# Attention row minima of the scores, held as minus SCALE times themselves, as the bias of the exponential

## The chip, the core and the metric

The kernel runs on one core of one Trainium2 chip. The metric is the device time of one execution, in microseconds (us). A core has engines that run side by side and wait for each other by semaphores: TensorE (PE, with its weight loads as PEld), VectorE (DVE), ScalarE (ACT), GpSimd (POOL) and the queue SP that issues DMAs.

## The reference, cut to what matters

A decoder trunk of two layers, 512 positions, width 1024. Each layer has three parallel mixers (an SSD scan, an S5 scan, and multi-head latent attention). The change touches the attention alone, in which each of 16 heads computes:

```python
sc = (einsum('bqhd,bkhd->bhqk', qn, k_nope) + einsum('bqhr,bkr->bhqk', qr, k_r)) * scale   # scale = 96 ** -0.5
sc = where(kpos[None, :] <= qpos[:, None], sc, NEG_INF)
pr = softmax(sc, axis=-1)
o  = einsum('bhqk,bkhd->bqhd', pr, v)
```

## The kernel before, in words

`mla` works through 16 heads in order. For a head, `attend_qk` makes the scores in four query blocks of 128 rows; by causality block qb has (qb + 1) x 128 keys. Each block is three matmuls into a PSUM bank (`mm3`, lines 61 to 63, tile `aux`), then one reduction on VectorE (line 612) that adds the mask `cmask`, writes the scores to the SBUF tile `sc`, and accumulates the row maximum into one column of `mx`. In the trace the reduction is a custom operation followed by a short read of its accumulator. After four blocks, one VectorE operation (line 617, through the helper at line 73) makes `nm` = -SCALE x `mx`, and four exponentials on ScalarE (line 619, helper at line 66) turn `sc` into exp(SCALE x sc + nm), with the row sums into `rs`.

`attend_v` follows for the same head: ten transposes on TensorE (line 634), evictions that split each result into a high part on ScalarE (`ph`) and a low part on VectorE (`pl`, helper line 78), and the matmuls with the values (lines 644 to 647). `values` then halves and adds (tile `tmp`) and, for each second head, multiplies with the gate (`keep` from `tmp` and `keep`, line 78).

Between the heads the loop also issues the next pair's query and key projections (weights are split into `wh` on ScalarE and `wl` on VectorE or GpSimd; `qh`, `ql`, `kh`, `kl` are splits of results) and steps of `s5_prep` through `fill`. The latter keep GpSimd in runs of products (`pw`, `pv`, helper line 81) and TensorE in small matmuls (`pm`, `pM`, `pk`).

Tiles in PSUM are few: `aux` has three banks for scores, transposes and values together. The order on each engine isn't the order of the text: a planner (`schedule_with_timeline_sim=True` at the end of the file) places each instruction by priority in the order of the text and by its own simulated times, and the engines then run these lists in order. `align` reserves pad columns, so that tiles behind it start at chosen places; tiles are padded to 32 bytes a partition.

Of the kernel before, what the change touches and what calls it, by code (L numbers as in the profile page):

```python
# [9 lines left out]
F32 = mybir.dt.float32  # L10
F32R = mybir.dt.float32r
I32 = mybir.dt.int32
AF = mybir.ActivationFunctionType
ALU = mybir.AluOpType
# [6 lines left out]
P = 128  # L21
# [4 lines left out]
SCALE = 96.0 ** -0.5  # L26
# [8 lines left out]
class Trunk:  # L35
# [563 lines left out]
    def attend_qk(self, mp, q, k, h):  # L599

        nc = self.nc
        mx, nm = (mp.tile([P, 4], F32, name=x, tag=x, bufs=2) for x in ("mx", "nm"))
        if h == 0:
            self.align(mp, 32)
        scs = []
        for qb in range(4):
            n = (qb + 1) * P
            qs = slice(qb * P, qb * P + P)
            ps = self.bank()
            self.mm3(ps[:, :n], q[0][0:96, qs], q[1][0:96, qs], k[0][0:96, :n], k[1][0:96, :n], True, True)  # L610
            sc = mp.tile([P, n], F32, name=f"sc{qb}", tag=f"sc{qb}", bufs=2)
            nc.vector.tensor_tensor_reduce(  # L612
                out=sc, in0=ps[:, :n], in1=self.cmask[:, 512 - n:512], op0=ALU.add, op1=ALU.max,
                scale=1.0, scalar=-3.0e38, accum_out=mx[:, qb:qb + 1],
            )
            scs.append(sc)
        self.ts(nm, mx, -SCALE, None, ALU.mult)
        for qb, sc in enumerate(scs):
            self.act_(sc, sc, AF.Exp, scale=SCALE, bias=nm[:, qb:qb + 1], accum_out=self.rs[:, qb, h:h + 1])
        return scs  # L620

    def attend_v(self, mp, scs, v):
# [604 lines left out]
```

## Time and profile before

| what | before |
| --- | --- |
| median of 3 runs | 2001.6 us (2001.11, 2001.6, 2006.5) |
| the profiled execution, its own time | 1999.34 us |
| its span, first to last instruction | 1997.5 us |
| TensorE busy | 1883.4 us, 94% |
| VectorE busy | 1448.1 us, 72% |
| ScalarE busy | 941.1 us, 47% |
| GpSimd busy | 645.6 us, 32% |
| mean granted TensorE clock | 0.965 of full |

The profile is of one execution. Busy time is the time in which an engine ran an instruction; the granted clock is the share of TensorE's full clock (2.4 GHz) that the chip allowed, and its other level is 0.5 (1.2 GHz). In the timeline a bracket behind an instruction gives the time for which its engine had been idle, and what ended that.

### The profile page before, as it was taken

The page shows a single profiled execution, that of the slowest core. Times are in us where ns is not written, and L with a number is a line of the kernel's source. Part 1 is how long each engine was busy: PE and PEld are TensorE (multiplying, and loading weights), DVE is VectorE, ACT ScalarE, POOL GpSimd, SP SyncE. Part 2 cuts the span into 40 slices and gives each one's busy share as a digit, 9 for nine tenths or more (in the row PEclk, how much of TensorE's full clock was granted, in tenths as well). Part 3 has the DMA queues.
Part 4 walks back from the last instruction along what each step waited for, and adds up shares of the span by engine and source line. Part 5 has one row for each costly group of instructions (what it writes and reads, how often), then busy time and mean ns, then how long its engine had stood idle before and what let it go on. Part 6 is the DMA issues. An engine that isn't in the chain of part 4 may idle for free.

```text
span 1997.5 us, 27806 instructions
## 1 busy us (share of the span) xinstructions
PE 1883.4 (94%) x9688; PEld 1530.5 (77%) x9688; DVE 1448.1 (72%) x2845; ACT 941.1 (47%) x1743; POOL 645.6 (32%) x743
## 2 busy tenths in 40 slices
PE   7897999899999989999998999998999999999998
PEld 5685777687887778888876777776878887788887
DVE  6866667699999857744579666677999996666443
ACT  4364556522555545543333655564235563555431
POOL 1855467301233201201118556672013331012010
PEclk9898999899999999999998999998999999899999
DMA  5333244232312266345223333342232224662541
GB/s 159 94 115 86 88 116 121 74 120 81 131 64 73 70 172 182 106 132 177 96 84 88 112 104 111 91 140 83 96 122 78 75 74 111 182 173 85 166 130 42
DMA packets 132605, 219.96 MB, mean 110 GB/s; under 512 B 36208, under 2 KB 75760, under 8 KB 131952
## 3 DMA queue, kind: packets, MB, share of 16 engines
q1 hardware_dynamic: 132464, 218.19, 36.0%
q8 instruction: 76, 1.25, 0.2%
q14 instruction: 65, 0.53, 0.1%
HBM read 182.08 MB, written 31.33 MB: 107 GB/s over the span
## 4 chain that ended last, share of the span: by engine, by line
PE 59%; DVE 24%; DMA 8%; POOL 3%; ACT 3%; issue 2%; SPq 1%; DVEq 0%; POOLq 0%; ACTq 0%
PE mm L116 13%; PE mm L117 13%; PE mm L119 12%; DVE wl L78 4%; DMA wf<-in_w_in 3%; DVE keep L69 3%; PE mm L61 2%; PE mm L62 2%; PE mm L63 2%; DVE ms L894 2%; DVE sc_t L891 2%; PE pk L385 2%; DVE ms L893 1%; PE aux L61 1%; PE aux L62 1%
## 5 line engine op out<-in xcount | busy, mean ns | idle before, releaser
L116 PE MATMUL mm<-hh,wh 128*128 128x512 f32 (+1 forms) x1232 | 500.9, 407 | 16.0 <-DVE ql L78 8.8
L117 PE MATMUL mm<-hl,wh 128*128 128x512 f32 (+1 forms) x1232 | 493.5, 401 | 0.0
L66 ACT ACTIVATE wh<-wf 128x1024 fp32r<-128x1024 f32 (+1 forms) x294 | 291.4, 994 | 422.9 <-PE mm L117 232.7
L78 DVE TENSOR_TENSOR wl<-wf,wh 128x1024 fp32r<-128x1024 f32 (+1 forms) x243 | 297.0, 1227 | 180.6 <-ACT wh L66 151.9
L119 PE MATMUL mm<-hh,wl 128*128 128x512 f32 (+1 forms) x1232 | 315.4, 393 | 3.8 <-DVE wl L78 3.8
L116 PEld LDWEIGHTS mm<-hh,wh 128*128 128x128 f32 (+1 forms) x1232 | 237.3, 193 | 77.9 <-DVE ql L78 9.9
L117 PEld LDWEIGHTS mm<-hl,wh 128*128 128x128 f32 (+1 forms) x1232 | 236.7, 192 | 50.0 <-issue 1.9
L119 PEld LDWEIGHTS mm<-hh,wl 128*128 128x128 f32 (+1 forms) x1232 | 227.7, 187 | 53.3 <-DVE wl L78 4.6
L81 POOL TENSOR_TENSOR mg<-mg,tmp 128x512 f32<-128x512 f32 x32 | 77.4, 2420 | 461.4 <-DVE tmp L78 244.0
L81 POOL TENSOR_TENSOR wl<-wf,wh 128x1024 fp32r<-128x1024 f32 (+1 forms) x51 | 109.0, 2138 | 291.2 <-PE mm L119 185.9
L116 PE MATMUL mm<-ah,wh 128*128 128x512 f32 x512 | 200.6, 394 | 0.0
L117 PE MATMUL mm<-al,wh 128*128 128x512 f32 x512 | 199.8, 391 | 0.0
L119 PE MATMUL mm<-ah,wl 128*128 128x512 f32 x512 | 127.6, 390 | 0.0
L116 PEld LDWEIGHTS mm<-ah,wh 128*128 128x128 f32 x512 | 96.5, 189 | 21.6 <-issue 1.8
L117 PEld LDWEIGHTS mm<-al,wh 128*128 128x128 f32 x512 | 96.3, 188 | 20.6 <-DVE keep L78 0.5
L119 PEld LDWEIGHTS mm<-ah,wl 128*128 128x128 f32 x512 | 95.7, 188 | 19.5
L612 DVE CUSTOM_DVE_ANT_0 sc<-aux,cmask 128x128 f32<-128x128 f32 (+3 forms) x128 | 60.3, 485 | 50.2 <-PE aux L63 48.4
L81 POOL TENSOR_TENSOR pv<-pq,ar 128x288 f32<-128x288 f32 x64 | 56.7, 906 | 86.3 <-PE pk L385 69.8
L66 ACT ACTIVATE sc<-sc,nm 128x128 f32<-128x128 f32 (+3 forms) x128 | 70.3, 553 | 28.7 <-DVE nm L73 28.7
L78 DVE TENSOR_TENSOR pl<-aux,ph 128x512 fp32r<-128x512 f32 (+1 forms) x96 | 54.7, 593 | 25.6 <-ACT ph L66 25.2
L69 DVE SCALAR_TENSOR_TENSOR keep<-mm,cw,keep 128x511 f32<-128x511 f32 (+2 forms) x96 | 71.0, 740 | 2.1 <-ACT keep L66 1.5
L66 ACT ACTIVATE tmp<-mm 128x512 f32<-128x512 f32 x76 | 44.8, 593 | 58.5 <-PE mm L63 32.3
(344 smaller groups left out, 4083.4 us busy)
## 6 DMA issues: line engine op xcount, KB each, us to landing
wf<-in_w_in SPq DMA_DIRECT2D x156, 512.0 KB
odr<-pv SPq DMA_DIRECT2D x64, 128.0 KB
wf<-in_w_c SPq DMA_DIRECT2D x16, 512.0 KB
wf<-in_w_a SPq DMA_DIRECT2D x16, 512.0 KB
wf<-kpad SPq DMA_DIRECT2D x128, 64.0 KB
wf<-odr SPq DMA_DIRECT2D x16, 512.0 KB
wf<-in_w_glu SPq DMA_DIRECT2D x16, 512.0 KB
wf<-in_w_b SPq DMA_DIRECT2D x16, 512.0 KB
```

Of the source, the lines that this page charges most:

```text
L61: mm(out, ah, bh, start=start, stop=False)
L62: mm(out, ah, bl, start=False, stop=False)
L63: mm(out, al, bh, start=False, stop=stop)
L66: self.nc.scalar.activation(out, in_, func, **kw)
L69: self.nc.vector.scalar_tensor_tensor(out, in0, s, in1, op0, op1)
L78: self.nc.vector.tensor_tensor(out, a, b, op)
L81: self.nc.gpsimd.tensor_tensor(out, a, b, op)
L116: mm(ps[:m], wh[:, o(i)], bh, start=i == 0, stop=False)
L117: mm(ps[:m], wh[:, o(i)], bl, start=False, stop=False)
L119: mm(ps[:m], wl[:, o(i)], bh, start=False, stop=i == k - 1)
L385: nc.tensor.matmul(pk.rearrange("p g k -> p (g k)"), bbp[b % 2][:, q:q + 4].rearrange("p g h -> p (g h)"), v1[:, :, 0:8].rearrange("p g k ...
L612: nc.vector.tensor_tensor_reduce(out=sc, in0=ps[:, :n], in1=self.cmask[:, 512 - n:512], op0=ALU.add, op1=ALU.max, scale=1.0, scalar=-3.0e3 ...
```

## The change

The reduction at line 612 now takes the minimum of -SCALE x (score + mask) and writes the scores scaled in that way. The row minima (`mn`) are the bias that the exponential needs, so the operation that made `nm` is gone, and the exponential's scale is -1. `mn` has eight columns, of which four are used; the pad behind it grows from 32 to 48 columns.

```diff
     def attend_qk(self, mp, q, k, h):
 
         nc = self.nc
-        mx, nm = (mp.tile([P, 4], F32, name=x, tag=x, bufs=2) for x in ("mx", "nm"))
+
+        mn = mp.tile([P, 8], F32, name="mn", tag="mn", bufs=2)
         if h == 0:
-            self.align(mp, 32)
+            self.align(mp, 48)
         scs = []
         for qb in range(4):
             n = (qb + 1) * P
@@ -610,13 +611,12 @@
             self.mm3(ps[:, :n], q[0][0:96, qs], q[1][0:96, qs], k[0][0:96, :n], k[1][0:96, :n], True, True)
             sc = mp.tile([P, n], F32, name=f"sc{qb}", tag=f"sc{qb}", bufs=2)
             nc.vector.tensor_tensor_reduce(
-                out=sc, in0=ps[:, :n], in1=self.cmask[:, 512 - n:512], op0=ALU.add, op1=ALU.max,
-                scale=1.0, scalar=-3.0e38, accum_out=mx[:, qb:qb + 1],
+                out=sc, in0=ps[:, :n], in1=self.cmask[:, 512 - n:512], op0=ALU.add, op1=ALU.min,
+                scale=-SCALE, scalar=3.0e38, accum_out=mn[:, qb:qb + 1],
             )
             scs.append(sc)
-        self.ts(nm, mx, -SCALE, None, ALU.mult)
         for qb, sc in enumerate(scs):
-            self.act_(sc, sc, AF.Exp, scale=SCALE, bias=nm[:, qb:qb + 1], accum_out=self.rs[:, qb, h:h + 1])
+            self.act_(sc, sc, AF.Exp, scale=-1.0, bias=mn[:, qb:qb + 1], accum_out=self.rs[:, qb, h:h + 1])
         return scs
```

## Rows read from the trace of the kernel before

**Rows 1.** The page, part 1: busy us of each engine, share, instructions.

```profile
PE 1883.4 (94%) x9688; PEld 1530.5 (77%) x9688; DVE 1448.1 (72%) x2845; ACT 941.1 (47%) x1743; POOL 645.6 (32%) x743
```

**Rows 2.** Windows: stretch, length, busy us (instructions) of each engine, clock, DMA.

```profile
250.00:390.00 140.00, 129.02 (x662) 103.16 (x661) 96.15 (x200) 84.08 (x209) 86.04 (x130) 0.91 0.37 106
390.00:1000.00 610.00, 595.48 (x3111) 484.45 (x3111) 458.54 (x834) 271.83 (x404) 111.84 (x67) 0.99 0.37 116
```

**Rows 3.** Tile nm: ns shortest/median/longest; idle us, times; line: busy us, mean ns.

```profile
L73 DVE TENSOR_SCALAR nm<-mx x32: 150/171/4473, 117.9 to 1357.1; 128x4 f32<-128x4 f32 x32
...
  DVE nm L73: 28.7, 15
...
L73 DVE TENSOR_SCALAR nm<-mx 128x4 f32<-128x4 f32 x32 | 23.2, 724 | 0.2
```

**Rows 4.** Timeline, head 15 of layer 0: start us, us, engine, operation, [idle before].

```profile
371.98 3.19 DVE L73 TENSOR_SCALAR nm<-mx 128x4 f32<-128x4 f32 x1
...
374.51 0.63 POOL L81 TENSOR_TENSOR pw<-pbb,ar 128x256 f32<-128x256 f32 x1
...
375.82 0.58 PE L645 MATMUL aux<-pl,v 128*64 128x384 f32 x1 [2.32 <-DVE pl L78]
```

**Rows 5.** Timeline, head 15 of layer 1.

```profile
1357.07 3.20 DVE L73 TENSOR_SCALAR nm<-mx 128x4 f32<-128x4 f32 x1
...
1360.92 0.39 PE L645 MATMUL aux<-pl,v 128*64 128x384 f32 x1 [2.79 <-DVE pl L78]
```

**Rows 6.** Timeline, head 12 of layer 0; the last row is layer 1.

```profile
324.72 1.02 DVE L73 TENSOR_SCALAR nm<-mx 128x4 f32<-128x4 f32 x1
...
325.77 0.40 ACT L66 ACTIVATE sc<-sc,nm 128x128 f32<-128x128 f32 x1 [1.24 <-DVE nm L73]
...
327.97 0.84 ACT L66 ACTIVATE ph<-aux 128x512 fp32r<-128x512 f32 x2
...
329.33 0.39 PE L645 MATMUL aux<-pl,v 128*64 128x384 f32 x1 [1.00 <-DVE pl L78]
...
1315.29 0.39 PE L645 MATMUL aux<-pl,v 128*64 128x384 f32 x1 [1.01 <-DVE pl L78]
```

**Rows 7.** Windows at half clock behind the TensorE gaps of rows 4 to 6.

```profile
331.40:338.20 6.80, 6.62 (x20) 5.19 (x21) 6.57 (x19) 4.42 (x13) 3.50 (x6) 0.50 0.34 95
...
375.80:379.20 3.40, 3.38 (x16) 3.28 (x16) 2.86 (x7) 3.21 (x10) 0.15 (x1) 0.50 0.09 31
1317.80:1321.20 3.40, 3.40 (x10) 2.27 (x10) 3.34 (x8) 2.09 (x8) 1.13 (x2) 0.51 0.43 159
1362.20:1369.00 6.80, 6.71 (x23) 4.37 (x22) 4.17 (x9) 5.05 (x14) 0.59 (x2) 0.50 0.04 9
```

**Rows 8.** Lines by shape; tile sc (ns shortest/median/longest); TensorE's waits (us, times, longest).

```profile
L66 ACT ACTIVATE sc<-sc,nm 128x512 f32<-128x512 f32 x32 | 22.7, 710 | 0.0
...
L612 DVE CUSTOM_DVE_ANT_0 sc<-aux,cmask x128: 273/484/692, 112.9 to 1355.5; 128x128 f32<-128x128 f32 x32, 128x256 f32<-128x256 f32 x32, 128x384 f32<-128x384 f32 x32, 128x512 f32<-128x512 f32 x32
...
L69 DVE SCALAR_TENSOR_TENSOR keep<-mm,cw,keep 128x511 f32<-128x511 f32 x32 | 23.7, 740 | 1.5 <-ACT keep L66 1.5
...
PE aux L634 <- DVE mx L612: 6.9, 6, 2.5
```

**Rows 9.** Gate products on VectorE: tile keep; TensorE's timeline behind two held ones.

```profile
L78 DVE TENSOR_TENSOR keep<-tmp,keep x16: 682/1056/4871, 150.7 to 1372.0; 128x512 f32<-128x512 f32 x16
...
156.39 0.80 PE L116 MATMUL mm<-hh,wh 128*128 128x512 f32 x1 [4.25 <-DVE ql L78]
...
1253.96 0.69 PE L634 MATMUL aux<-ident,sc 128*128 128x128 f32 x2 [2.52 <-DVE mx L612]
```

**Rows 10.** Timeline, the longest nm (head 5 of layer 1), GpSimd and VectorE.

```profile
1183.18 4.47 DVE L73 TENSOR_SCALAR nm<-mx 128x4 f32<-128x4 f32 x1
...
1186.93 0.69 POOL L81 TENSOR_TENSOR pv<-bc,ai 128x288 f32<-128x288 f32 x1
...
1187.90 1.21 DVE L78 TENSOR_TENSOR wl<-wf,wh 128x1024 fp32r<-128x1024 f32 x1
```

## The prediction

> **What bounds the kernel now.** I read the engine totals first [rows 1]: TensorE is busy 94% of the span, VectorE 72%, ScalarE 47%. A shorter VectorE or ScalarE list is therefore worth something only where TensorE stands still. Next the stretches by stage [rows 2]: outside attention TensorE is busy 595.48 of 610.00 us, but in the second half of layer 0's attention it is idle for 140.00 - 129.02 = 11.0 us, and its mean granted clock is 0.91 of full. The whole change lies in attention, so the question is which of those idle microseconds belong to the step that goes.
>
> That step is `nm`, the 128x4 scaling of the row maxima, 32 times (16 heads, two layers). The answer for that tile [rows 3] is the main reading: the median is 171 ns, the shortest 150 ns, the longest 4473 ns; ScalarE stood idle for 28.7 us until one of them ended. A 128x4 operation has no reason of its own to take 4 us. The timeline around the longest ones tells why [rows 4, 10]: `nm` reads and writes SBUF, GpSimd was in an unbroken run of `pw` and `pv` products, and `nm` ended as one of the last of them ended (375.14 against 375.17; 1187.62 against 1187.65). The score reduction, which has one input in PSUM, shows no such stretching: the longest of its 128 takes 692 ns, for the largest shape [rows 8]. Of the 23.2 us that `nm` takes in all [rows 3], 32 x 0.171 = 5.5 are medians; the other 17.7 are waits, at 14 of the 32 places.
>
> One rule can be weighed against this. The Trainium skill, "SBUF — State Buffer", section "SBUF: two separate sides", says that VectorE and GpSimd take a shared port pair by an exclusive lock for a whole instruction, and that an operation with two SBUF inputs contends as well. The kind of wait agrees with the trace, its length less so: the 3.19 us of [rows 4] outlast several GpSimd instructions of 0.6 to 0.8 us, where the page's rule would give one. By one GpSimd instruction for each of 14 holds the whole effect would be at most 14 x 0.7 = 9.8 us of VectorE time, an estimate; the rows give 17.7.
>
> **The change part by part.**
>
> *`nm` goes.* Where does TensorE wait for it? Following each hold to the next idle entry of TensorE I find four places.
> - Head 15, layer 0 [rows 4]: `nm` sits ahead of `pl` on VectorE, and TensorE's values matmul waits 2.32 us for `pl`. Without `nm`, `pl` can start when its hi part is written, and the wait closes.
> - Head 15, layer 1 [rows 5]: the same order, 2.79 us.
> - Head 12, layers 0 and 1 [rows 6]: ScalarE's first exponential waits 1.24 us for `nm`; behind the four exponentials stands the `ph` eviction (327.97), and TensorE waits 1.00 and 1.01 us for what follows. The 1.24 us cover the 1.00.
> Sum: 2.32 + 2.79 + 1.00 + 1.01 = 7.1 us. The other ten holds have no TensorE gap of their own: the largest, 4.47 us [rows 10], ran beside matmuls that had their operands, so I count it at nothing. What covers it are projections; with those gone it would cost up to 4.47.
>
> What is late next? At head 15 the transposes need the exponentials, which now start behind `nm`; free of it they start when ScalarE has done its evictions, some 3 us sooner, and take at most 4 x 0.71 = 2.8 us [rows 8]. I allow 1 us of the 7.1 to come back there, as the lower end (6.1).
>
> *The clock.* Each of these gaps lies in or just ahead of a stretch at granted clock 0.50, that is 1.2 instead of 2.4 GHz [rows 7]. TensorE did 6.62 + 3.38 + 3.40 + 6.71 = 20.1 us of work in the four; at full clock that is half, so up to 10.1 us hang on the gaps. Other idle entries stand close by (the `pM` and `pml` waits of head 12 and 15), so some of these stretches can stay. Ends: 0 and 10.1. I take the middle, 5.0, since nothing in the trace says which of two neighbouring gaps lowered the clock.
>
> *The reduction with min and a scale of -SCALE.* The trace has no such reduction. It has the same custom operation with max and a scale of 1, up to 692 ns; the nearest two-step operation with a PSUM input and a per-partition factor takes 740 for 128x511 [rows 8]. So 0 to +50 ns each, 128 instructions, at most 6.4 us of VectorE time. TensorE waited six times, 6.9 us, for these reductions at line 634 [rows 8]: 6 x 0.05 = 0.3 us. A gain has no ground, as the operation count stays. I take 0: the multiply already stands in the old instruction, by 1.0.
>
> *The exponentials* keep form, count and an immediate scale: 0, plus or minus nothing that a row would show. They depend on one reduction now where `nm` made each wait for all four. This can move three of four ahead of the last reduction, off the block on ScalarE that delayed `ph` in [rows 6]. In heads 1 to 14 it is hidden by the projection and `s5_prep` matmuls that lie between a head's exponentials and its transposes; I count nothing beyond the 1.00 above. A new wait takes the place of the old: the exponential on its own reduction. Behind it on ScalarE stand the same `ph` and `wh` evictions as behind `nm`, and the reduction ends before `nm` did, so the wait is no longer than now.
>
> *The pad* (48 for 32 columns) only restores the place of the tiles behind it: two tags of two buffers become one, and it moves no work. I cost it at 0.
>
> *Order.* The planner places instructions from its own simulated times, so a dropped step and earlier exponentials can reorder the four engines through attention. I take 0 for it, and its ends, 13.6 us less and 20 us more, come from rivals D and C below.
>
> Sum against the profiled execution: 1999.3 - 7.1 - 5.0 = 1987.2. That execution was 2.3 us under the median of 2001.6, so the same gain from the median gives 1989.5. With the ends: 1995.5 (6.1 and no clock) to 1984.4 (7.1 and 10.1).
>
> **The rivals.**
>
> *B, the wait passes on.* VectorE's next instructions with two SBUF inputs meet the same GpSimd runs. For: the `wl` split follows soon behind the 4.47 us hold [rows 10], and the products of attention output and gate (`keep` from `tmp` and `keep`) are held as long as 4.87 us [rows 9]. Against: at head 15 the next on VectorE are two `pl`, which read PSUM. If only head 12 gains, with its clock half used, it is 2.0 + 2.5 less than now, about 1997; if nothing, 2001.6. By the Trainium skill's section above, with its lock on operations with two SBUF inputs, this would be the outcome.
>
> *C, slower: a new order lays the gate products into GpSimd's runs.* Place: the 16 products of [rows 9] that close a pair of heads. Five of 16 are now held for over 3 us, three in layer 0 and two in layer 1, though both layers run the same code; so the draw does move with order. Price: the first and the last of the five TensorE waits behind them are 4.25 and 2.52 us [rows 9], in the middle 3.4, and a half-clock stretch of 6.8 us [rows 7] costs 3.4 more: 6.8 each. Two more held ones eat the 12.1 us; three more give 1989.5 + 20.4 = 2010. It decides from three on.
>
> *D, the same draw the other way.* Two of the five go free: 1989.5 - 13.6 = 1976.
>
> That the change doesn't do what it says (exponentials still placed behind the fourth reduction) costs nothing here: all 7.1 us come from `nm` itself, and this falls within the first case.
>
> **How the numbers follow.** A change of 0.3%, 6.0 us, is about what a measurement of this kernel can tell from none; faster is under 1995.6, slower over 2007.6. Chances: A, the forecast, 0.43, at 1989.5 (own range 1984 to 1995.5, all faster); B 0.27, at 1997 to 2002, within 0.3%; C 0.20, at 2010, slower; D 0.10, faster. So faster 0.53, same 0.27, slower 0.20. The range runs from 1977, which leaves out half of D, to 2010, which leaves out half of C: 0.15 left out. Cases of both signs hold chance, so the own range of A stands beside it.
>
> **What would show it.** Right: no `nm`; VectorE busy about 23 us less; the 2.3 and 2.8 us entries of TensorE at head 15 and the 1.0 us ones at head 12 gone; fewer half-clock stretches in attention, the mean clock there over 0.91. ScalarE's 28.7 us idle until `nm` becomes a smaller sum until the reduction. Wrong: the reduction at more than 740 ns for 128x512; new long `keep` products or `wl` splits beside GpSimd runs (B, C); as many half-clock stretches as now with the gaps gone, which would leave only 7.1 us; or TensorE's idle time in attention as large as before, in other places.

## The result, and the profile after

The changed kernel takes 2019.6 us against 2001.4 us for the kernel before, measured side by side: a ratio of 1.0091 (95% interval 1.0068 to 1.0113). It is slower by 0.9%, where 1989.5 us with a range of 1977 to 2010 was forecast. The profiled execution took 2019.9 us, its span is 2018.1 us; the span of before was 1997.5. Of the runs told of below, one of the six executions of mix_order took 7616.2 us: the 2019.9 us given for it leave that one out, the 2020.7 us of the expectations do not.

The operations are as forecast. Engine totals of the changed kernel (page, part 1), to be read against [rows 1]:

```profile
PE 1877.5 (93%) x9688; PEld 1524.4 (76%) x9688; DVE 1434.8 (71%) x2813; ACT 941.8 (47%) x1743; POOL 651.0 (32%) x743
```

The 32 `nm` are gone (2845 instructions on VectorE less 2813). VectorE is busy 13.3 us less, not 23. TensorE even works 5.9 us less (1883.4 to 1877.5), so all of the loss is idle time: span less busy was 114.1 us and is 140.6.

Reduction and exponentials of the changed kernel (answers on the tiles sc and mn: ns shortest/median/longest; idle us, times), to be read against [rows 8] and [rows 3]:

```profile
L613 DVE CUSTOM_DVE_ANT_0 sc<-aux,cmask x128: 273/484/692, 110.9 to 1361.3; 128x128 f32<-128x128 f32 x32, 128x256 f32<-128x256 f32 x32, 128x384 f32<-128x384 f32 x32, 128x512 f32<-128x512 f32 x32
...
  DVE mn L613: 29.1, 25
```

The reduction with min and a scale costs exactly what the one with max did: 273, 484 and 692 ns in both. ScalarE's idle time in front of the exponentials is not smaller (28.7 us for `nm`, 29.1 for `mn`), only cut into more pieces (15, now 25).

TensorE's waits in the changed kernel (us in all, times, longest us):

```profile
PE mm L116 <- DVE ql L78: 14.7, 6, 4.8
...
PE pM L378 <- DVE pml L78: 9.6, 5, 5.5
...
PE aux L634 <- DVE mn L613: 4.4, 7, 1.4
...
PE aux L645 <- DVE pl L78: 0.7, 2, 0.4
```

The last row is the forecast itself: the waits for `pl` at heads 15 and 12 [rows 4 to 6] were 7.1 us and are 0.7 (at line 644 they rose from 0.3 to 2.0). But others came: for `ql`, for `pml`, and more below.

Windows by stage, first of the changed kernel, then (a run told of below) of the same operations in the order of the kernel before. The eight rows of each are, for layer 0 and then layer 1: attention (first score product to first `w_c` product); the `w_c` products and the start of the S5 scan; the SSD heads; S5, GLU and `w_b`. Columns as in [rows 2]; TensorE's idle time is the length less its busy time.

```profile
109.71:385.50 275.79, 248.00 (x1289) 201.68 (x1287) 179.13 (x362) 160.97 (x397) 160.33 (x235) 0.94 0.36 102
385.50:516.69 131.19, 124.07 (x531) 97.92 (x530) 113.93 (x358) 37.74 (x53) 10.46 (x5) 0.98 0.31 105
516.69:681.91 165.22, 163.19 (x903) 131.70 (x903) 151.15 (x257) 94.62 (x155) 55.11 (x37) 1.00 0.25 79
681.91:966.81 284.90, 274.26 (x1525) 225.59 (x1524) 164.94 (x187) 126.10 (x167) 44.07 (x20) 0.99 0.49 144
...
1104.99:1381.91 276.92, 247.59 (x1299) 202.05 (x1298) 178.34 (x362) 160.11 (x398) 157.95 (x238) 0.95 0.36 102
1381.91:1512.98 131.07, 125.16 (x532) 99.11 (x531) 113.57 (x360) 37.69 (x53) 10.71 (x5) 0.97 0.32 107
1512.98:1680.33 167.35, 160.60 (x871) 129.72 (x871) 154.47 (x244) 92.60 (x152) 53.63 (x35) 1.00 0.24 76
1680.33:1967.28 286.95, 278.03 (x1557) 229.46 (x1556) 169.33 (x199) 127.19 (x170) 44.47 (x21) 0.99 0.48 142
```

```profile
111.48:387.89 276.41, 248.32 (x1293) 201.62 (x1291) 181.45 (x363) 160.47 (x400) 160.71 (x235) 0.94 0.35 102
387.89:516.44 128.55, 126.37 (x549) 101.02 (x549) 116.45 (x363) 39.85 (x54) 11.75 (x6) 0.97 0.35 117
516.44:685.26 168.82, 163.56 (x914) 131.92 (x914) 159.76 (x260) 94.30 (x157) 54.46 (x38) 1.00 0.21 70
685.26:963.23 277.97, 270.63 (x1491) 222.68 (x1490) 159.84 (x178) 122.79 (x162) 41.78 (x19) 0.99 0.51 148
...
1100.63:1370.66 270.03, 249.28 (x1308) 201.39 (x1306) 180.72 (x367) 160.37 (x403) 163.72 (x240) 0.96 0.37 106
1370.66:1499.40 128.74, 125.47 (x549) 100.20 (x548) 116.67 (x364) 40.59 (x55) 11.08 (x7) 0.98 0.35 117
1499.40:1660.60 161.20, 161.20 (x914) 132.38 (x914) 155.49 (x261) 93.78 (x156) 53.17 (x37) 1.00 0.22 73
1660.60:1937.12 276.52, 269.83 (x1492) 222.87 (x1490) 159.25 (x178) 122.84 (x162) 40.27 (x18) 0.99 0.50 147
```

TensorE's idle time out of these rows, layer 0 + layer 1, in us (the rest is the start of a layer and the end):

| stage | changed kernel | same operations, order of before | difference |
|---|---|---|---|
| attention | 27.8 + 29.3 | 28.1 + 20.8 | 8.2 |
| `w_c`, start of the scan | 7.1 + 5.9 | 2.2 + 3.3 | 7.5 |
| SSD heads | 2.0 + 6.8 | 5.3 + 0.0 | 3.5 |
| S5, GLU, `w_b` | 10.6 + 8.9 | 7.3 + 6.7 | 5.5 |
| rest | 42.1 | 41.8 | 0.3 |

The counts in brackets show that matmuls moved between stages as well (1557 against 1492 in the last row). The planner drew the whole order anew, far behind the place of the edit, and the loss is spread over four stages. One row of it is conspicuous, from the timeline of SyncE's queue and VectorE behind layer 1's attention (start us, us, engine, operation, [idle before]):

```profile
1390.60 0.55 SPq L401 DMA_DIRECT2D msd<-pmo  x1
...
1398.40 0.33 SPq L887 DMA_DIRECT2D ms<-msd  x1
...
1394.99 1.22 DVE L78 TENSOR_TENSOR wl<-wf,wh 128x1024 fp32r<-128x1024 f32 x1 [0.59 <-PE mm L119]
1406.47 0.28 DVE L891 TENSOR_TENSOR sc_t<-sc,ms 128x64 f32<-128x64 f32 x1 [10.26 <-DMA ms<-msd]
```

VectorE, which takes its list in order, reaches the S5 scan 10.26 us before the scan's data. In both layers together this wait is 20.5 us, and it was 0.6 us in the kernel before (tile ms of the changed kernel, then of before; idle us, times):

```profile
  DMA ms<-msd: 20.5, 2
```

```profile
  DMA ms<-msd: 0.6, 1
```

In the instruction lists, 37 and 36 matmuls (layers 0 and 1) lie between the last product with v and the last `pM` matmul of the S5 preparation, from which those data come; before there were 12 and 12. And only 7 and 8 VectorE instructions lie between the last `pmo` and the scan; before there were 23 and 23 (the expectations below count rows of the lists, 20 there, of which some stand for two or three instructions).

### The profile page after: what moved, and what is told of

Same layout as the page of the kernel before. It is cut to its first block, busy times and chain, and to the rows that moved or that the text cites. A ratio compares the mean times of both kernels' runs of the same rounds, so it can differ in the third digit from the quotient of the medians.

```text
span 2018.1 us, 27792 instructions
## 1 busy us (share of the span) xinstructions
PE 1877.5 (93%) x9688; PEld 1524.4 (76%) x9688; DVE 1434.8 (71%) x2813; ACT 941.8 (47%) x1743; POOL 651.0 (32%) x743
## 4 chain that ended last, share of the span: by engine, by line
PE 51%; DVE 27%; DMA 11%; issue 4%; ACT 3%; POOL 2%; SPq 1%; DVEq 0%; ACTq 0%; POOLq 0%
PE mm L116 12%; PE mm L117 11%; PE mm L119 11%; DVE wl L78 4%; DVE keep L69 3%; DMA wf<-in_w_in 3%; PE mm L62 2%; PE mm L61 2%; PE mm L63 2%; DVE ms L894 2%; DMA msd<-pmo 2%; DVE ms L893 1%; DVE sc_t L891 1%; PE aux L61 1%; DMA sf<-sdr 1%
## 5 line engine op out<-in xcount | busy, mean ns | idle before, releaser
L116 PE MATMUL mm<-hh,wh 128*128 128x512 f32 (+1 forms) x1232 | 501.2, 407 | 32.8 <-DVE ql L78 14.7
L119 PE MATMUL mm<-hh,wl 128*128 128x512 f32 (+1 forms) x1232 | 322.6, 395 | 7.6 <-DVE wl L78 7.6
L66 ACT ACTIVATE sc<-sc,mn 128x128 f32<-128x128 f32 (+3 forms) x128 | 71.3, 558 | 29.3 <-DVE mn L613 29.1
```

The costliest lines, as they stand in the source:

```text
L66: self.nc.scalar.activation(out, in_, func, **kw)
L116: mm(ps[:m], wh[:, o(i)], bh, start=i == 0, stop=False)
L119: mm(ps[:m], wl[:, o(i)], bh, start=False, stop=i == k - 1)
```

## The experiments

Two theories stood at the start: **the operations** cost something, or **the order** does. Within the second, the late scan was my first candidate.

**The arithmetic alone.** In the kernel before, the reduction takes min and -SCALE, and `nm` multiplies by 1.0:

```diff
-                ... op0=ALU.add, op1=ALU.max, scale=1.0, scalar=-3.0e38, accum_out=mx[:, qb:qb + 1],
+                ... op0=ALU.add, op1=ALU.min, scale=-SCALE, scalar=3.0e38, accum_out=mx[:, qb:qb + 1],
-        self.ts(nm, mx, -SCALE, None, ALU.mult)
+        self.ts(nm, mx, 1.0, None, ALU.mult)
-            ... AF.Exp, scale=SCALE, bias=nm[:, qb:qb + 1]
+            ... AF.Exp, scale=-1.0, bias=nm[:, qb:qb + 1]
```

> The kernel before with the new arithmetic alone: the reduction takes the minimum and multiplies by -SCALE, the exponential has a scale of -1, and nm stays as minima x 1.0. The instruction lists of the five queues have the order of before. Theory T (the loss of the change is the planner's new order, not the operations): 2001 +- 3 us, nm 32 times with the same long waits beside GpSimd, the reduction at about 685 ns for 128x512. Rival R (minimum and scale make the reduction or the exponential slower): reduction over 700 ns, and part or all of the 18 us, 2008 to 2020.

1998.97 us, ratio 0.9992 (0.9980 to 1.0004), with the instruction order of the kernel before on all queues. The new arithmetic costs nothing.

**`nm` in another layout**, `mx` and `nm` taking every second column of eight:

```diff
+        mx, nm = (mp.tile([P, 8], F32, name=x, tag=x, bufs=2)[:, ::2] for x in ("mx", "nm"))
```

> The kernel before, in its order, with mx and nm in every second column of eight, so that nm has a strided input and output. It asks what the waits of nm are worth with the order held. If a strided nm doesn't wait for GpSimd's runs: nm at most 0.25 us each, VectorE about 18 us less busy, TensorE's waits of 2.32 and 2.79 us (head 15) and 1.00 and 1.01 us (head 12) gone, 7 to 17 us less: 1984 to 1995 us. If the clock gives nothing back, 1994; if something else is late next, 1997 to 2001. If it still waits, nothing is learnt and the time is 2001.

1999.27 us, ratio 0.9995 (0.9984 to 1.0006). The layout doesn't free `nm` (the longest is 3202 ns, ScalarE idle 25.6 us for it), so this run says nothing of what the hold is worth.

**The late scan, first tries.** In the changed kernel, gate projections and `w_c` products are queued on TensorE behind the last `pM` matmul:

```diff
+            with tc.issue_after(self.last_pm.ins):
                 self.gates_ahead(l, 2, 2)
...
+                with tc.issue_after(self.last_pm.ins):
                     for m in range(8):
                         self.merge(l, 2, a["w_c"], acts, m)
```

> The changed kernel, with the gate projections and the w_c merges that follow attention queued on TensorE behind the last matmul of s5_prep (an edge of order only). Theory T: the late scan load is the loss; VectorE's wait for ms from msd falls from 20.5 us to under 5 us in all, and the time from 2019.6 to 1998 to 2006 us. Rival (the loss lies in attention or elsewhere in the new order): the wait falls and the time stays over 2014.

2015.11 us, ratio 1.0072 (1.0057 to 1.0087). The load went out sooner, but the planner put the scan still further forward on VectorE: it waited 16.6 us there, with the split `r` behind it, and TensorE waited 19.6 us for `r`. So this run does not price the wait. Next, the other way round, in the kernel before: one gate projection traced ahead of the S5 preparation's last step, and this step's matmuls behind it.

> The kernel before, with the last matmuls of s5_prep queued on TensorE behind one gate projection (24 matmuls) that is traced ahead of them, as the planner did in the changed kernel. Nothing else of the change. Theory T: the scan load goes out 5 to 12 us later in each layer, VectorE waits for it 5 to 10 us in each, and the time is 2008 to 2022 us. Rival: 2001 +- 4 us, as the scan isn't on the path.

1999.55 us, ratio 0.9999 (0.9986 to 1.0012). The planner placed that gate earlier too, and the load didn't come late (1.7 us of waits): inconclusive.

**The order held fixed.** These kernels trace the program twice: the planner's order of the kernel before is read off, and in the program that runs every instruction is put behind its predecessor of that order on its engine, by an edge that costs no semaphore:

```diff
+                last = {}
+                for k in order:                       # the order of the kernel before, without nm
+                    i = seq[k]
+                    if i.engine in last:
+                        tc.add_manual_dep(i, last[i.engine], ...NoSync...)
+                    last[i.engine] = i.name
```

> The changed kernel's operations in the order of the kernel before: on each of the five queues every instruction is queued behind the one that it follows in the order of the kernel before, with the 32 nm instructions left out, so that nothing but the change's own operations tells it from the kernel before. Theory (no operation costs anything, all of the loss is the redrawn order): the step of the prediction on nm holds here, 1989.5 us (1983 to 1996), ratio 0.991 to 0.998, the PE waits on plh of heads 15 and 12 gone. Rival 1 (nm's waits were beside other work anyway): 1998 to 2003, ratio 1.000. Rival 2 (something in the changed operations themselves costs on the chip): 2008 us or more, ratio over 1.004.

1990.89 us, ratio 0.9945 (0.9926 to 0.9964). That is the time that was forecast: the same operations as in the changed kernel, 28.7 us faster, by the order alone. Totals of this run and TensorE's waits:

```profile
PE 1872.2 (94%) x9688; PEld 1521.9 (77%) x9688; DVE 1437.5 (72%) x2813; ACT 939.5 (47%) x1743; POOL 648.1 (33%) x743
```

```profile
PE pM L379 <- DVE pml L79: 11.2, 8, 3.8
PE aux L661 <- DVE mn L616: 10.1, 8, 2.5
...
PE aux L671 <- DVE pl L79: 0.3, 2, 0.2
```

The waits for `pl` are gone (7.1 to 0.3), but those for `pml` rose from 4.6 to 11.2 and those for the reduction from 6.9 [rows 8] to 10.1. A part of that rise is scatter from one execution to the next: in nm_kept, where `nm` still stands in the way, they were 7.6 and 8.3. Idle time in all is 1987.6 - 1872.2 = 115.4 us, where it was 114.1. The gain stands in the busy time: attention's 1293 and 1308 matmuls took 253.06 and 255.94 us in before and take 248.32 and 249.28 here, at a mean granted clock of 0.94 and 0.96 instead of 0.92 and 0.93. The windows of before for these two stretches:

```profile
111.71:391.40 279.69, 253.06 (x1293) 205.10 (x1291) 184.70 (x379) 160.89 (x400) 157.96 (x235) 0.92 0.35 101
...
1100.35:1377.90 277.55, 255.94 (x1308) 206.37 (x1306) 187.53 (x383) 161.44 (x403) 163.36 (x240) 0.93 0.36 105
```

The same with `nm` left in its place on VectorE, where nobody reads it:

> The order of the kernel before on all five queues, nm among it in its old place on VectorE, but nobody reads nm: the reductions give the minima of minus SCALE times the scores, and the exponentials take these as their bias. Beside after_order (1990.9 us, nm gone as well) it tells which half of the gain is whose. If the exponentials' wait for nm is what cost (the step of the prediction at heads 15 and 12): 1988 to 1994 us. Rival (the 23.2 us that nm holds VectorE, which delays the splits behind it, is what cost): 1998 to 2003 us.

1995.29 us, ratio 0.9963 (0.9951 to 0.9975), between the two answers offered: about two thirds of the gain come with the exponentials' freedom, the rest with VectorE's; the intervals overlap, so the shares are rough. `nm` is still held there, for up to 3218 ns, and most of TensorE's waits for `pl` behind it are still there too:

```profile
PE aux L671 <- DVE pl L79: 5.4, 4, 2.8
```

Yet the attention is nearly as short as in after_order. Its windows in both layers, of nm_kept (the exponentials wait for `nm`) and then of exp_free (they don't):

```profile
110.61:389.94 279.33, 250.74 (x1293) 202.79 (x1291) 185.66 (x379) 161.04 (x400) 159.20 (x235) 0.93 0.34 101
1101.89:1376.25 274.36, 253.51 (x1308) 204.23 (x1306) 184.87 (x383) 160.96 (x403) 161.72 (x240) 0.94 0.36 105
```

```profile
110.05:387.17 277.12, 248.05 (x1293) 201.16 (x1291) 184.82 (x379) 160.41 (x400) 160.91 (x235) 0.94 0.36 102
1102.33:1373.14 270.81, 249.38 (x1309) 201.82 (x1307) 185.80 (x383) 160.42 (x403) 164.20 (x240) 0.96 0.37 106
```

Busy time of the two layers is 509.0 us in before, 508.3 in nm_strided, 504.3 in nm_kept, 497.4 in exp_free and 497.6 in after_order; idle time is 48.2, 48.6, 49.4, 50.5 and 48.8. So the attention's gain comes with the exponentials and stands in TensorE's busy time, at a higher granted clock; it does not need the gaps for `pl` to close. Why the clock was lower while the exponentials waited for `nm` is not shown.

**Which part of the order costs.** Only what stands behind the attention keeps the order of before; the attention and the S5 preparation are left to the planner:

> The changed kernel, where only what stands behind the attention (from the gates and the row sums to the output projection, both layers) is queued in the order of the kernel before; the attention and what runs beside it stay in the order that the planner draws for the change. Theory (the loss is made in the stages behind the attention, by the scan standing at the head of VectorE's queue and by the redrawn SSD and S5 stages): 1988 to 1997 us, with the DVE wait for ms<-msd under 3 us in all. Rival (the redrawn attention itself hands its work over late, and the stages behind it only show that): 2005 to 2020 us, the wait for ms<-msd still some 20 us.

2019.9 us, ratio 1.0087 (1.0066 to 1.0108). The theory put the loss behind the attention, and it fell: with those stages in the old order nothing is won back. VectorE waits 20.2 us for `ms`. Now the S5 preparation keeps its old order as well, and only the attention is the planner's:

> The changed kernel, where the S5 preparation and all that stands behind the attention are queued in the order of the kernel before, and the attention itself is left to the planner: 12 and 14 matmuls between the last product with v and the last pM matmul, 20 VectorE instructions between the last pmo and the scan. It tells apart which part of the redrawn attention stage costs in mix_order (2020.7 us). Theory (the end of the S5 preparation, hence the scan's data, is late; the redrawn attention itself costs nothing): 1986 to 1997 us, wait for ms<-msd under 3 us. Rival (the attention's own new order costs): 2005 us or more with no such wait.

2002.83 us, ratio 1.0010 (1.0000 to 1.0020), wait for `ms` 1.9 us. Neither of the two answers that I had offered: the end of the S5 preparation is worth 2019.9 - 2002.8 = 17.1 us beside these lists, and the attention's own new order 2002.8 - 1990.9 = 11.9. By the ratios, each taken against executions of the kernel before at its side, it is some 15 and 13 us, and each can be off by about 5. The second sits in layer 1, whose attention lasts 288.0 us here against 270.0.

**The price of a late scan**, in the order of before: the load is issued twice.

```diff
         nc.sync.dma_start(ms, msd...)
+        nc.sync.dma_start(ms[:, :, :, 1:], msd[:, :, :, :, 1:]...)
```

> The changed kernel in the order of the kernel before (1990.9 us) with the scan's load ms<-msd issued a second time right behind the first, so that the scan's data land some 8 us later in each layer and nothing else moves. Theory (VectorE bounds the stretch from the scan to the last SSD head, so a late load there is paid nearly in full): VectorE waits 14 to 18 us in all for ms, the time is 2001 to 2009 us. Rival (the wait is caught up by TensorE's own work before the SSD heads, the loss of the changed kernel comes from its other lists): 1989 to 1996 us with the same wait.

2010.43 us, ratio 1.0055 (1.0036 to 1.0075). The answer on tile ms (idle us, times) and TensorE's waits:

```profile
  DMA ms<-msd: 28.8, 4
```

```profile
PE mm L117 <- DVE mg L70: 16.2, 2, 8.4
```

While VectorE stands in front of the scan, the sums `mg` behind it in its list stand too, and TensorE runs out of PSUM for the `w_c` products. In these lists a late scan costs 19.5 us for 28.2 us more of waiting. Both are more than expected (14 to 18 us of waiting, 2009 us at most): the wait came to 14.4 us a layer, where the second load was to add some 8.

**The late scan mended in the changed kernel's order**, with the edges of after_fix and the scan queued behind the last split of the attention's output:

```diff
+                with tc.issue_after(self.last_tt.ins):
                     self.s5_scan(l, sp)
```

> The changed kernel in the planner's order, but for two edges per layer: the gate projections and the w_c products are queued behind the last pM matmul (as in after_fix), and the scan is queued on VectorE behind the last split of the attention's output. 9 matmuls then lie between the last product with v and the last pM matmul, and 30 VectorE instructions between the last pmo and the scan. Theory: the wait for ms<-msd falls under 3 us and TensorE's wait for r (9.84 us in after_fix) goes; 1990 to 2003 us. Rival (other lists of the redraw cost by themselves): 2008 us or more although both waits are gone.

2007.61 us, ratio 1.0035 (1.0022 to 1.0048). The wait for `ms` is gone altogether, TensorE still waits 7.8 us for `r`, and 16.7 us remain to after_order. A late scan is not the whole loss.

**What makes the planner redraw.** For the planner alone, the first three exponentials of a head stand behind the fourth reduction, as `nm` had made them stand:

```diff
             ex = self.act_(sc, sc, AF.Exp, scale=-1.0, bias=mn[:, qb:qb + 1], ...)
+            if qb < 3:
+                self.tc.add_manual_dep(ex.ins, red.ins.name, ...NoSync..., reason="hold")
```

> The changed kernel, and for the planner alone the first three exponentials of a head stand behind the fourth reduction, as nm made them stand (an edge of order, no semaphore on the chip). In the lists that come out, 12 matmuls lie between the last product with v and the last pM matmul in both layers (before 12 and 12, after 37 and 36), and 20 to 22 VectorE instructions between the last pmo and the scan (before 20, after 7). Theory (the exponentials' new freedom in the planner's time makes it draw the tail of the attention so that the scan comes before its data): 1986 to 1996 us, ratio 0.992 to 0.998, VectorE's wait for ms<-msd under 3 us in all. Rival (any redraw of these lists loses some 20 us, the kernel before being a lucky draw): 2010 us or more.

1989.22 us, ratio 0.9945 (0.9933 to 0.9956). With this edge the changed operations are faster than both kernels, at the time forecast for them. The lists show 12 and 12 matmuls and 26 and 23 VectorE instructions where the changed kernel has 37 and 36, and 7 and 8, and VectorE's wait is (tile ms of after_hold):

```profile
  DMA ms<-msd: 0.3, 1
```

The other way round, `nm` is there but unread, and the planner is free:

> The same operations as in exp_free, in the order that the planner draws by itself: nm is there, and the exponentials don't wait for it in the planner's time either. 39 and 37 matmuls lie between the last product with v and the last pM matmul (before 12 and 12, after 37 and 36), and 20 and 5 VectorE instructions between the last pmo and the scan. Theory (it is the exponentials' freedom in the planner's time that redraws the tail of the attention, not the absence of nm): 2005 to 2024 us. Rival (it is the absence of nm): 1988 to 2001 us.

2034.60 us, ratio 1.0163 (1.0145 to 1.0181), above even the 2024 us that I had set as the upper end. The absence of `nm` is not needed for a slow order; freedom of the exponentials is enough. The same with each exponential behind `nm` for the planner:

> nm_dead (2034.6 us) with one thing more: for the planner alone each exponential stands behind nm, which nobody reads (an edge of order, no semaphore on the chip). The operations are those of nm_dead and of exp_free (1995.3 us); the order is drawn anew by the planner and is neither of theirs: 12 and 12 matmuls between the last product with v and the last pM matmul, 20 and 18 VectorE instructions between the last pmo and the scan. It repeats the pair of after and after_hold with nm in place. Theory (the exponentials' freedom in the planner's time is what makes it draw a slow order): 1990 to 2001 us. Rival (after_hold was a lucky draw, and a redrawn order loses 20 us or more as a rule): 2010 us or more.

2003.82 us, ratio 1.0011 (0.9995 to 1.0028): 30.8 us faster than nm_dead, the second pair with that difference, though above the 2001 that I had set. Against exp_free, the same operations in the old order at 0.9963, this new order loses some 10 us. So a redrawn order is not neutral in itself.

**The late scan alone, in the changed kernel's own lists.** The load takes data that are there from the start, so these kernels leave the state of the S5 scan out of the result:

```diff
-        nc.sync.dma_start(ms, msd...)
+        nc.sync.dma_start(ms..., self.a["w_c"][l, 0:4]...)
```

> The changed kernel in the order of the kernel before (after_order, 1990.9 us), but the scan's load takes 2 MB of w_c, which are there from the start, in place of msd, so that neither the load nor the queue of SyncE waits for the S5 preparation; the state of the S5 scan is left out of the computation by that. It is the control for after_early: VectorE waits 0.6 us for the load in after_order, so the theory and its rival both expect 1987 to 1994 us.

> The changed kernel in its own order on all five queues (2019.6 us), with the load of order_early (the state of the S5 scan is left out of the computation): only the lateness of the scan's data is taken away. Theory (about half of the 29 us between after and after_order is the late scan, as mix_order less prepmix_order says, 17.9 us, the rest the order of the attention, 11.9 us): VectorE waits under 2 us for ms, 2000 to 2006 us. If the late scan is the whole loss: 1988 to 1994 us. If the wait is only where another delay shows: 2014 us or more.

> nm_dead in its own order (2034.6 us), with the load of order_early (the state of the S5 scan is left out of the computation). Its scan stands on VectorE 20 instructions behind the last pmo in layer 0 and 5 in layer 1. Theory: what nm_dead loses beside after (15 us) is lost in the same way, so this comes out within 5 us of after_early. If another list of its order is what costs: 2015 us or more.

1990.65, 2019.80 and 2030.13 us, ratios 0.9955 (0.9939 to 0.9972), 1.0102 (1.0085 to 1.0119) and 1.0153 (1.0133 to 1.0174). The second and third don't price the late scan: VectorE still waited 15.2 and 8.6 us, since the load stands behind the last `msd` store on its queue (in layer 1 of after_early it went out at 1396.22 us, the store at 1393.80); that its tile lies on tiles of the S5 preparation, which hold it too, is argued from the layout and not traced. The third waits less than the second and takes 10.3 us longer, so what nm_dead loses beside the changed kernel is, for the most part, not the scan. To price it, the scan was given a small tile of its own:

```diff
+            ms = self.msp.tile([P, 2, 32, 2], F32, name="ms", tag="ms")      # two columns in turn
+            nc.sync.dma_start(ms..., self.a["w_c"][l, 0][:, 0:128])          # two places earlier on its queue
...
-            s, d = ms[:, :, :, c], ms[:, :, :, c + 1]
+            s, d = ms[:, :, :, c % 2], ms[:, :, :, (c + 1) % 2]
```

> Control for after_ring, in the order of the kernel before (after_order, 1990.9 us): the scan runs on a small tile of its own, two columns that it uses in turn, loaded early from w_c; its 252 VectorE operations stay in number, shape and place, and the store behind it takes hh. So the scan waits for nothing from the S5 preparation, and its state is left out of the computation; the 2 MB load goes. VectorE waits 0.6 us for that load in after_order, so all theories expect 1984 to 1994 us.

> The changed kernel in its own order on all five queues (2019.6 us), with the scan of order_ring, whose state is left out of the computation. In after_early the load stayed behind the last msd store on the queue of SyncE and behind the tiles of the S5 preparation in SBUF, so VectorE still waited 15.2 us for it; here nothing of that is left. Theory (the late data of the scan are most of the loss): VectorE waits under 1 us there, 1988 to 2000 us. If they are half of it (17.9 of 29 us, by mix_order less prepmix_order): 2000 to 2006 us. Rival (the lateness costs nothing in these lists, the loss is in their order): 2012 us or more.

1980.46 us, ratio 0.9893 (0.9876 to 0.9910), and 2000.34 us, ratio 1.0000 (0.9987 to 1.0012). No wait for `ms` is left in either. The control gains 10.4 us by itself, below what I had set for it, since the scan's operations are shorter on the small tile (last section); so the two must be compared with each other. They differ by 19.9 us, where the kernels with the real scan differ by 28.7: the late scan is 8.8 us of the loss. By the four intervals this difference of differences can be off by some 7 us; the 7.5 us of idle time in the `w_c` row of the table above agree with it. Windows of after_ring, layer 1, attention to S5:

```profile
1094.90:1371.96 277.06, 247.61 (x1300) 202.57 (x1298) 178.81 (x362) 159.97 (x398) 157.73 (x238) 0.95 0.36 102
1371.96:1494.13 122.17, 122.17 (x532) 98.57 (x531) 101.77 (x360) 39.73 (x54) 10.48 (x5) 0.98 0.32 106
1494.13:1660.52 166.39, 160.42 (x872) 129.83 (x872) 155.68 (x244) 91.81 (x151) 53.64 (x35) 1.00 0.22 70
1660.52:1947.80 287.28, 277.62 (x1557) 229.15 (x1556) 168.97 (x199) 126.89 (x170) 44.42 (x21) 0.99 0.48 141
```

The second row has no idle time left; attention (29.5 us), SSD heads (6.0) and S5 (9.7) idle as in the changed kernel (29.3, 6.8, 8.9). These 20 us are the order of the lists without the late scan.

## Why the prediction was wrong

*What bounds the kernel, and the holds on `nm`:* the holds were read rightly, and so was the size of the gain. Where the order is that of before, taking the exponentials off `nm` and `nm` off VectorE gives a ratio of 0.9945, which is 1990.6 us of 2001.6; 1989.5 was forecast for it. It did not come by the path that was forecast, as the steps on `nm`, the clock and the exponentials show.

*`nm` goes, 7.1 us of gaps:* the gaps closed as named (0.3 us left in after_order), but "what is late next" was mis-sized. I allowed 1 us to come back. In the profiled executions the waits for `pml` and for the reduction grew by 6.6 and 3.2 us, and the sum of idle time did not fall (114.1 to 115.4; 117.6 in nm_kept).

*The clock, 5.0 us:* mis-sized the other way. TensorE's busy time fell by 1883.4 - 1872.2 = 11.2 us from before, just over the upper end of 10.1, and by 5.1 from nm_kept (1877.3 us), which has the order and, within its interval, the time of before. In the attention alone it fell by 11.4 and 6.7 us. So the busy time is the whole gain there, where the sum had it as the smaller part; that the two errors cancel is luck. Nor did this gain hang on the gaps for `pl`: exp_free has it with 5.4 of the 7.1 us still open.

*Reduction 0, pad 0:* right. The reduction's 273/484/692 ns did not move, and nm_kept gives 0.9992.

*Exponentials 0:* right for their own time, wrong for their freedom. By the working, exp_free, where `nm` stays on VectorE, keeps the 2.0 us of head 12 and, as in rival B, 2.5 us of clock: 4.5 us. It gained 7.4 (5.0 to 9.8 by its interval).

*Order 0, with ends of -13.6 and +20:* this is the step that failed, and that made the forecast miss. It was 28.7 us, outside its ends, and it carried the sign. I had taken it at 0 because the edit lies in attention, and had bounded it by the five held gate products alone. The planner, though, draws all lists from its own times, and what it drew lost 8.2 us in attention, 7.5 in `w_c`, 3.5 in the SSD heads and 5.5 in S5. The rows of before could have shown how much hung on the end of attention: VectorE waited 0.6 us for `ms<-msd` even there, so the scan had no time to spare.

*Which part set it off:* the line "they depend on one reduction now" for the exponentials, costed at nothing. On the chip that freedom is a gain (exp_free). In the planner's time it is what draws the slow order: with it 2019.6 and 2034.6, without it 1989.2 and 2003.8, for the same two sets of operations.

*Rival B, the wait passes on:* it was given "the same" and no loss, but its mechanism is in the changed kernel. VectorE's busy time fell by 13.3 us where `nm` had taken 23.2: other operations took 9.9 us longer. The largest rise is that of `pq`, an operation of the S5 preparation (lines by shape, before and then the changed kernel; busy us, mean ns):

```profile
L73 DVE TENSOR_SCALAR pq<-bc,sgn 128x128 f32<-128x128 f32 x16 | 10.9, 680 | 16.9 <-DMA bc<-in_s_bc 13.9 <-POOL pv L81 2.8
```

```profile
L73 DVE TENSOR_SCALAR pq<-bc,sgn 128x128 f32<-128x128 f32 x16 | 22.1, 1380 | 16.9 <-DMA bc<-in_s_bc 14.0 <-POOL pv L81 2.9
```

One place in layer 1, timeline of before and then of the changed kernel:

```profile
1286.99 0.41 DVE L73 TENSOR_SCALAR pq<-bc,sgn 128x128 f32<-128x128 f32 x1 [0.60 <-POOL pv L81]
```

```profile
1292.88 4.57 DVE L73 TENSOR_SCALAR pq<-bc,sgn 128x128 f32<-128x128 f32 x1
...
1296.73 0.63 POOL L81 TENSOR_TENSOR pw<-pbs,ai 128x256 f32<-128x256 f32 x1
1297.48 0.69 DVE L78 TENSOR_TENSOR ql<-mm,qh 64x512 fp32r<-64x512 f32 x1
...
1298.22 0.79 PE L116 MATMUL mm<-hh,wh 128*128 128x512 f32 x1 [4.78 <-DVE ql L78]
```

Before, `pq` came early in an unbroken run of GpSimd instructions (1285.13 to 1291.36) and took 0.41 us. Now it stands two reductions later and a little further into the same run, and ends 0.1 us behind the run's last product (1297.45 against 1297.36), and TensorE waits 4.78 us for `ql` behind it. Most of the rise of the waits for `ql` (8.8 to 14.7 us) is this one. It does not tell the slow order from the fast one, though: after_hold has it too (4.73 us, behind a `pq` of 4.52).

*Rival C, slower:* the sign was right and the mechanism wrong. The gate products, which it wanted held more often, are held less: median 1056 ns before [rows 9], 752 after, and three of 16 over 3 us where it was five.

*What stays open:* why an earlier exponential leads the planner to these lists, and why the order costs attention 8.2 us and S5 5.5, wait by wait. The late scan is put at some 9 us of the 29, within the 7 us either way given above; the rest is shown to be the order, not traced to single choices in it. Open too is why TensorE's clock in the attention was lower while the exponentials waited for `nm`.

## What to carry to other kernels

Where a planner lays out the instructions from its own times, an edit that frees an instruction is two changes, the operations and a new order. Cost them apart, bound the order by what other orders of the same kernel measured, and when a sound change measures slow, put the old order (or the old dependency, for the planner alone) back before giving it up: here that turned 2019.6 us into 1989.2.
Ahead of such an edit, look for transfers that land with no time to spare in front of an engine that takes its list in order; a step placed a few instructions too early stops all that is queued behind it.
When a wait on the path is removed, the idle time of the stage is the measure, not the one wait: here 6.8 us of gaps closed, 9.8 us opened beside them, and what was won stood in the busy time.

## What the runs showed of the hardware

A small VectorE operation with both tensors in SBUF can be held for several GpSimd instructions on end, not only for one. The three longest `nm` of before took 3.2 to 4.5 us, and the `pq` shown above 4.57 us, while seven GpSimd products of 0.28 to 0.78 us each began and ended. It is not held in every such run: the `pq` of 0.41 us in the kernel before ran inside one. The Trainium skill, "SBUF — State Buffer", section "SBUF: two separate sides", has the loser of the shared port pair blocked for one whole instruction of the other; the runs agree with the blocking and not with its length. Taking every second column does not lift it (nm_strided: 14 waits, longest 3202 ns, as with columns side by side in nm_kept).

The scan's operations depend on the step between their elements. Tile ms in the changed kernel, and then in order_ring, for one of the four operations (ns shortest/median/longest):

```profile
L892 DVE TENSOR_TENSOR sc_t<-sc,ms x126: 250/267/280, 410.0 to 1505.9; 128x64 f32<-128x64 f32 x126
```

```profile
L927 DVE TENSOR_TENSOR sc_t<-sc,ms x126: 211/218/229, 400.1 to 1467.8; 128x64 f32<-128x64 f32 x126
```

The same 128x64 elements, 64 floats apart in one and 2 apart in the other: 267 against 218 ns. The small tile lies at another place in SBUF as well; no run tells the place from the step. Over the 504 operations of the scan at some 50 ns that is about 25 us of VectorE's time, and the kernel with the small tile was 10.4 us faster, though its early load, and the 2 MB that it no longer moves, can have a part in that too. A scan that keeps its current column packed was not tried with the real data.

From store to use the scan's data take two hops of some 8 us: `msd` is stored at 1390.60, the load goes out at 1398.40, and VectorE starts at 1406.47.
